# A two-layer decoder trunk on one core: gate and up products of an FFN chunk in a PSUM bank each

## The chip, the core and the metric

The kernel runs on one core of a Trainium2 chip. Five engines of the core work side by side, each on its own list of instructions: TensorE (PE; its weight loads are listed as PEld), VectorE (DVE), ScalarE (ACT), GpSimd (POOL) and SyncE (SP, which issues the DMAs). They meet at semaphores. Matmul results go to PSUM, which the program uses as eight banks of 512 fp32 columns by 128 partitions. The metric is the device time of one execution in microseconds; the median of three runs is 998.04 us (997.99 to 998.23).

## The reference

A trunk of two layers works on x of 256 rows by 1024 columns in fp32. Each layer is FFN, mixer, FFN, each with a scaled residual and a layer norm:

```
def swiglu(x, w_gu, w_down):
    g, u = jnp.split(x @ w_gu, 2, axis=-1)
    return (jax.nn.silu(g) * u) @ w_down

x = layer_norm(ALPHA * x + 0.5 * swiglu(x, ffn_w_gu[l, 0], ffn_w_down[l, 0]), ...)
y = mixer_ab(...) if l % 2 == 0 else mixer_c(...)
x = layer_norm(ALPHA * x + y, ...)
x = layer_norm(ALPHA * x + 0.5 * swiglu(x, ffn_w_gu[l, 1], ffn_w_down[l, 1]), ...)
```

The FFN width is 2816: gate and up are 1024 x 2816 each, down is 2816 x 1024. The first mixer is attention beside a spatial gating unit, the second an mLSTM. The four FFNs are what the change touches.

## The kernel before, in words

Every fp32 operand of a large product is split into a high part (fp32r) and the rest, and a product is three matmuls, high by high, high by rest, rest by high (mm3, lines 119 to 122). Weights come from HBM as pages of 128 x 1024 fp32 (512 KB): SP loads a page into one of 6 raw buffers, ACT casts it to whi (line 92), DVE subtracts to get wlo (line 93), and both parts lie in rings of 9 pages. When TensorE is done with page n, w_done (line 86) splits page n + 9 and loads page n + 15.

An FFN begins with two or four tiles of 128 rows by 512 columns (gate 256, up 256), which are transposed afterwards (post, line 314). All the other columns go in chunks of 128 (chunk, line 327): 20 chunks in the first FFN, 18 in each of the others, 74 together. A chunk computes its gate product transposed, 128 columns by all 256 rows, with 8 x 3 = 24 matmuls out of one weight page (proj_t, line 255), then its up product with 24 more out of the next page. ACT takes Silu of the gate (line 332), DVE multiplies it by the up product (line 334), and ACT and DVE split the result hT into its two parts. Then come the down products into four banks with the tag a (out_proj, line 265) and the layer norm.

PSUM has three pools: four banks with the tag a, three with the tag m, one with the tag t. A tile of tag m is taken by bank_m (line 51), in turn; a tile takes a bank again when all readers of the bank's last tile are done. Gate and up of a chunk are the two halves of one such tile.

The code is written in one order, but a scheduler of the framework sets the order on each engine except SP (line 36): it lays the instructions out by priority and its own costs, and so may put matmuls of the next chunk ahead of those which it believes to wait. It also sets the semaphore waits, and treats two engines at one PSUM bank as dependent, also where they touch different columns.

Of the kernel before, what the change touches and what calls it, by code (L numbers as in the profile page):

```python
# [10 lines left out]
AF = mybir.ActivationFunctionType  # L11
OP = mybir.AluOpType
AX = mybir.AxisListType

P = 128
S = 256
# [14 lines left out]
def trunk(ctx, tc, W, xT_d, x_d, g_d, b_d, rope_d, id_d, idb_d, mk_d, tri_d, sel_d,  # L31
          sg_d, sb_d, sw_d, sbt_d, cw_d, wif_d, bif_d, hg_d, out_d):
    nc = tc.nc
# [11 lines left out]
    def bank(tag, bufs, shape=(P, 512), dt=F32):  # L45
        return psum.tile(list(shape), dt, tag=tag, name="ps_" + tag, bufs=bufs)
# [4 lines left out]
    def bank_m(shape=(P, 512)):  # L51
        return bank("m", 3, shape)

    def bank_t(shape=(P, 512)):
        return bank("t", 1, shape)

    def page(name, shape, dt=F32):
        n = 1
        for d in shape[1:]:
            n *= d  # L60
        v = pages.tile([P, 516], dt, tag="p2", name=name, bufs=PAGES)[:, 0:n]
        if len(shape) == 3:
            v = v.rearrange("p (a b) -> p a b", a=shape[1])
        elif len(shape) == 4:
            v = v.rearrange("p (a b c) -> p a b c", a=shape[1], b=shape[2])
        return v
# [19 lines left out]
    def w_done(n):  # L86
        del whi[n], wlo[n]
        w_split(n + RING)
        w_dma(n + RING + RAW)

    def split(src, hi, lo):
        nc.scalar.copy(out=hi, in_=src)  # L92
        nc.vector.tensor_tensor(out=lo, in0=src, in1=hi.bitcast(F32), op=OP.subtract)  # L93
# [3 lines left out]
    def spawn(gen):  # L97
        side.append([0, gen])
        return gen
# [7 lines left out]
    def tick():  # L107
        for e in list(side):
            e[0] -= 1
            if e[0] <= 0:  # L110
                step(e)

    def finish(gen):
        for e in list(side):
            if e[1] is gen:
                while e in side:
                    step(e)

    def mm3(out, lh, ll, rh, rl, start, stop):
        mm_(out=out, lhsT=lh, rhs=rh, start=start, stop=False)  # L120
        mm_(out=out, lhsT=lh, rhs=rl, start=False, stop=False)  # L121
        mm_(out=out, lhsT=ll, rhs=rh, start=False, stop=stop)  # L122
# [67 lines left out]
    def load_consts():  # L190
        nc.sync.dma_start(out=identb, in_=idb_d)
        nc.sync.dma_start(out=maskb, in_=mk_d)
        nc.sync.dma_start(out=tri, in_=tri_d)
        nc.sync.dma_start(out=sel, in_=sel_d)
        nc.sync.dma_start(out=cw, in_=cw_d)
        nc.sync.dma_start(out=bif, in_=bif_d)
# [44 lines left out]
    def proj(t, n0, release, out=None, js=range(4)):  # L241
        ps = out if out is not None else bank_m()
        for j in js:
            rh = whi[n0 + j].rearrange("p (a n) -> p a n", a=2)
            rl = wlo[n0 + j].rearrange("p (a n) -> p a n", a=2)
            for i in range(2):
                kc = 2 * j + i
                mm3(ps, xTh[:, kc, t * P:(t + 1) * P], xTl[:, kc, t * P:(t + 1) * P],
                    rh[:, i, :], rl[:, i, :], kc == 0, kc == 7)
            if release:  # L250
                w_done(n0 + j)
            tick()
        return ps

    def proj_t(n, ps):
        wh = whi[n].rearrange("p (k n) -> p k n", k=KC)
        wl = wlo[n].rearrange("p (k n) -> p k n", k=KC)
        for kc in range(KC):
            mm3(ps, wh[:, kc, :], wl[:, kc, :], xTh[:, kc, :], xTl[:, kc, :], kc == 0, kc == 7)
            if kc == 3:  # L260
                tick()
        w_done(n)
        tick()

    def out_proj(nk, n0, lhs, skew, k, scale, eps, last):
        acc = [[None, None], [None, None]]

        def one(c, t, release, hs=(0, 1)):
            n = n0 + c
            lh, ll = lhs(c, t)  # L270
            for h in hs:
                if acc[t][h] is None:
                    acc[t][h] = bank_a()
            for h in hs:
                mm3(acc[t][h], lh, ll, whi[n][:, h * 512:(h + 1) * 512], wlo[n][:, h * 512:(h + 1) * 512],
                    c == 0, c == nk - 1)
            if release:
                w_done(n)
            if 1 in hs:
                tick()  # L280

        for c in range(nk - skew):
            one(c, 0, False)
            one(c, 1, True)
        for c in range(nk - skew, nk):
            one(c, 0, False, (0,))
        ln0 = layer_norm(0, acc[0], scale, eps, k, last)
        next(ln0)
        for c in range(nk - skew, nk):
            one(c, 0, False, (1,))  # L290
        spawn(ln0)
        if last:
            segs = ((0, 512), (512, 256), (768, 256))
            accs = [acc[1][0], acc[1][1], bank_m()]
            ln1 = layer_norm(1, accs, scale, eps, k, last, segs)
            for i, (o, w) in enumerate(segs):
                for c in range(nk - skew, nk):
                    n = n0 + c
                    lh, ll = lhs(c, 1)
                    mm3(accs[i][:, 0:w], lh, ll, whi[n][:, o:o + w], wlo[n][:, o:o + w],  # L300
                        i == 2 and c == nk - skew, c == nk - 1)
                next(ln1)
            finish(ln0)
            return spawn(ln1)
        for c in range(nk - skew, nk):
            one(c, 1, True)
        finish(ln0)
        return spawn(layer_norm(1, acc[1], scale, eps, k, last))

    def ffn(n0, k, ln_prev, last=False):  # L310
        hT = {}
        head = 1 if ln_prev is None else 2

        def post(g, t, ps):
            hp = pages.tile([P, 2, 256], F32, tag="h", name="hp", bufs=3)
            nc.scalar.activation(out=hp[:, 0, :], in_=ps[:, 0:256], func=AF.Silu)
            nc.vector.tensor_tensor(out=hp[:, 1, :], in0=hp[:, 0, :], in1=ps[:, 256:512], op=OP.mult)
            yield 2
            pt = bank_t((P, 2, P))
            for c in range(2):  # L320
                nc.tensor.transpose(pt[:, c, :], hp[:, 1, c * P:(c + 1) * P], ident)  # L321
            q = page("hT", [P, 2, 2, P], F32R)
            for c in range(2):
                hT[2 * g + c, t] = (q[:, 0, c, :], q[:, 1, c, :])
            split(pt, q[:, 0], q[:, 1])

        def chunk(c):
            n = n0 + 4 * head + 2 * (c - 2 * head)
            ps = bank_m()
            hp = pages.tile([P, 2, 256], F32, tag="h", name="hp", bufs=3)  # L330
            proj_t(n, ps[:, 0:256])
            nc.scalar.activation(out=hp[:, 0, :], in_=ps[:, 0:256], func=AF.Silu)  # L332
            proj_t(n + 1, ps[:, 256:512])
            nc.vector.tensor_tensor(out=hp[:, 1, :], in0=hp[:, 0, :], in1=ps[:, 256:512], op=OP.mult)  # L334
            q = page("hT", [P, 2, S], F32R)
            split(hp[:, 1, :], q[:, 0], q[:, 1])
            for t in range(2):
                w = slice(t * P, (t + 1) * P)
                hT[c, t] = (q[:, 0, w], q[:, 1, w])

        if ln_prev is None:
            load_consts()
        gens = []
        if ln_prev is None:
            order = []
            ps = [bank_m(), bank_m()]
            for j in range(4):
                proj(0, n0, False, ps[0], (j,))
                proj(1, n0, True, ps[1], (j,))
            for t in range(2):  # L350
                gens.append(spawn(post(0, t, ps[t])))
        else:
            order = [(0, 0), (1, 0), (0, 1), (1, 1)]
        for g, t in order:
            if (g, t) == (0, 1) and ln_prev is not None:
                finish(ln_prev)
            ps = proj(t, n0 + 4 * g, t == 1)
            gens.append(spawn(post(g, t, ps)))
        for c in range(2 * head, FC):
            chunk(c)  # L360

        def lhs(c, t):
            if (c, t) not in hT:
                for e in gens:
                    finish(e)
            return hT[c, t]

        return out_proj(FC, n0 + 4 * FG, lhs, 7, k, 2.0 * ALPHA, 4.0 * EPS, last)
# [478 lines left out]
```

## Time and profile before

| | |
|---|---|
| median of 3 runs | 998.04 us |
| profiled execution, its own time | 998.46 us |
| its span | 996.5 us |
| PE busy | 981.1 us (98%) |
| DVE, ACT busy | 596.0 us (60%), 458.4 us (46%) |
| DMA | 183.01 MB, mean 184 GB/s |

The span runs from the first to the last instruction of the profile. Busy time of PE is the union of drawn matmuls, whose ends are modelled, so a matmul is drawn longer than the distance to the next one's start. Where PE loses time is seen in the distances between starts and in the idle time of PEld, the weight load ahead of each matmul.

### The profile page before, as it was taken

To read this page: it belongs to the slowest core of one execution; us is meant where nothing else is said; L and a number is where in the kernel's file an instruction comes from. 1 tells how busy PE (TensorE), PEld (TensorE's weight loads), DVE (VectorE), ACT (ScalarE), POOL (GpSimd) and SP (SyncE) were. 2 spreads that over 40 slices of the span, in tenths; PEclk is the share of its full clock that TensorE was granted. 3 is DMA by queue.
4 is the path that set the end of the run, shared out by engine and by line. 5 is a ranking of instruction groups with operands and counts; after the bars stand their busy time and mean duration, and the time that the engine had idled before them with its cause. 6 is when DMAs were issued, how large, how long until landed. Compare 5 with 4: busy or idle time off the path is not lost.

```text
span 996.5 us, 15539 instructions
## 1 busy us (share of the span) xinstructions
PE 981.1 (98%) x6212; PEld 863.5 (87%) x6212; DVE 596.0 (60%) x822; ACT 458.4 (46%) x664; POOL 23.8 (2%) x36
## 2 busy tenths in 40 slices
PE   8999999999999999999999999999999999999997
PEld 5999998887788999988889999888888789999886
DVE  5575554586768655554675555448767885555434
ACT  5464443346645444443354444324675454444420
POOL 0000000010000000000000000001000000000000
PEclk9999999999999999999999999999999999999999
DMA  8885556386336655566565555655634466555611
GB/s 298 295 277 180 181 186 192 118 284 199 118 113 225 215 187 184 176 190 190 166 221 182 180 183 170 194 186 198 209 125 130 136 225 212 184 171 179 197 48 42
DMA packets 52215, 183.01 MB, mean 184 GB/s; under 512 B 6192, under 2 KB 6832, under 8 KB 52016
## 3 DMA queue, kind: packets, MB, share of 16 engines
q1 hardware_dynamic: 52144, 182.04, 56.5%
q8 instruction: 48, 0.79, 0.3%
q14 instruction: 23, 0.19, 0.1%
HBM read 180.97 MB, written 1.05 MB: 183 GB/s over the span
## 4 chain that ended last, share of the span: by engine, by line
PE 94%; DVE 2%; issue 1%; ACT 1%; DMA 1%; POOL 0%; SPq 0%; DVEq 0%; ACTq 0%
PE ps_m L120 22%; PE ps_m L121 20%; PE ps_m L122 20%; PE ps_a L121 10%; PE ps_a L120 9%; PE ps_a L122 9%; DVE wlo L93 1%; PE ps_a L232 1%; DMA raw<-in_W 1%; PE ps_a L428 1%; POOL hrs L201 0%; ACT whi L92 0%; PE ps_a L465 0%; PE ps_t L321 0%; ACT hp L332 0%
## 5 line engine op out<-in xcount | busy, mean ns | idle before, releaser
L92 ACT CAST whi<-raw 128x1024 fp32r<-128x1024 f32 (+1 forms) x325 | 339.9, 1050 | 402.7 <-PE ps_m L121 227.1
L93 DVE TENSOR_TENSOR wlo<-raw,whi 128x1024 fp32r<-128x1024 f32 (+1 forms) x325 | 394.5, 1221 | 153.6 <-ACT whi L92 151.7
L120 PE MATMUL ps_m<-xTh,whi 128*128 128x256 f32 x1280 | 366.4, 286 | 3.1 <-DVE qkc L637 1.4
L121 PE MATMUL ps_m<-xTl,whi 128*128 128x256 f32 x1280 | 357.6, 280 | 0.0
L122 PE MATMUL ps_m<-xTh,wlo 128*128 128x256 f32 x1280 | 347.2, 279 | 0.0
L120 PEld LDWEIGHTS ps_m<-xTh,whi 128*128 128x128 f32 x1280 | 240.4, 188 | 18.6 <-ACT hp L332 16.2
L121 PEld LDWEIGHTS ps_m<-xTl,whi 128*128 128x128 f32 x1280 | 240.7, 188 | 0.4 <-issue 0.2
L122 PEld LDWEIGHTS ps_m<-xTh,wlo 128*128 128x128 f32 x1280 | 236.3, 188 | 0.3 <-issue 0.3
L120 PE MATMUL ps_a<-whi,hT 128*128 128x512 f32 (+1 forms) x352 | 138.2, 393 | 0.0
L121 PE MATMUL ps_a<-wlo,hT 128*128 128x512 f32 (+1 forms) x352 | 138.1, 392 | 0.0
L122 PE MATMUL ps_a<-whi,hT 128*128 128x512 f32 (+1 forms) x352 | 137.9, 392 | 0.0
L334 DVE TENSOR_TENSOR hp<-hp,ps_m 128x256 f32<-128x256 f32 x74 | 31.2, 421 | 159.3 <-PE ps_m L122 159.3
L120 PE MATMUL ps_m<-whi,xTh 128*128 128x512 f32 x240 | 98.3, 411 | 2.6 <-ACT whi L92 2.5
L121 PE MATMUL ps_m<-wlo,xTh 128*128 128x512 f32 x240 | 96.7, 403 | 0.5 <-DVE wlo L93 0.5
L122 PE MATMUL ps_m<-whi,xTl 128*128 128x512 f32 x240 | 95.9, 400 | 0.0
L122 PEld LDWEIGHTS ps_a<-whi,hT 128*128 128x128 f32 x352 | 66.1, 188 | 15.2
L120 PEld LDWEIGHTS ps_a<-whi,hT 128*128 128x128 f32 x352 | 66.1, 188 | 14.9
L121 PEld LDWEIGHTS ps_a<-wlo,hT 128*128 128x128 f32 x352 | 66.2, 188 | 14.8
L120 PEld LDWEIGHTS ps_m<-whi,xTh 128*128 128x128 f32 x240 | 45.7, 191 | 13.3 <-ACT whi L92 3.8
L121 PEld LDWEIGHTS ps_m<-wlo,xTh 128*128 128x128 f32 x240 | 45.9, 191 | 10.8 <-DVE wlo L93 1.2
L122 PEld LDWEIGHTS ps_m<-whi,xTl 128*128 128x128 f32 x240 | 45.7, 190 | 10.5
L210 DVE SCALAR_TENSOR_TENSOR xn<-xn,ps_a 128x512 f32<-128x512 f32 x24 | 16.0, 684 | 37.0 <-PE ps_a L122 36.9
(189 smaller groups left out, 583.2 us busy)
## 6 DMA issues: line engine op xcount, KB each, us to landing
raw<-in_W SPq DMA_DIRECT2D x323, 512.0 KB, 4.3
gb<-in_g SPq DMA_DIRECT2D x6, 512.0 KB, 4.2
gb<-in_b SPq DMA_DIRECT2D x6, 512.0 KB, 5.1
xn<-in_x SPq DMA_DIRECT2D x1, 1024.0 KB
out<-xn SPq DMA_DIRECT2D x4, 256.0 KB, 2.1
xt<-in_xT SPq DMA_DIRECT2D x3, 256.0 KB, 7.6
raw<-in_W SPq DMA_DIRECT2D x2, 256.0 KB, 3.5
swt<-in_sw SPq DMA_DIRECT2D x2, 256.0 KB, 7.9
```

The lines of the kernel that those rows point to most:

```text
L92: nc.scalar.copy(out=hi, in_=src)
L93: nc.vector.tensor_tensor(out=lo, in0=src, in1=hi.bitcast(F32), op=OP.subtract)
L120: mm_(out=out, lhsT=lh, rhs=rh, start=start, stop=False)
L121: mm_(out=out, lhsT=lh, rhs=rl, start=False, stop=False)
L122: mm_(out=out, lhsT=ll, rhs=rh, start=False, stop=stop)
L210: nc.vector.scalar_tensor_tensor(out=sl, in0=sl, scalar=scale, in1=acc[i], op0=OP.mult, op1=OP.add)
L232: nc.tensor.transpose(pt[:, c, :], sl[:, c * P:(c + 1) * P], ident)
L334: nc.vector.tensor_tensor(out=hp[:, 1, :], in0=hp[:, 0, :], in1=ps[:, 256:512], op=OP.mult)
L428: mm_(out=dst, lhsT=qk[0, t][:, c, :], rhs=kp[c][:, :, 0:nk * P], start=True, stop=False, skip_group_check=True)
```

## The change

A chunk takes two tiles of the tag m in place of one, each of 128 partitions by 256 columns, the gate product in the first, the up product in the second. Silu and the multiplication read the new tiles. The pool still has three banks. Line numbers behind the change move: the multiplication on line 334 becomes line 335.

```
         def chunk(c):
             n = n0 + 4 * head + 2 * (c - 2 * head)
-            ps = bank_m()
             hp = pages.tile([P, 2, 256], F32, tag="h", name="hp", bufs=3)
-            proj_t(n, ps[:, 0:256])
-            nc.scalar.activation(out=hp[:, 0, :], in_=ps[:, 0:256], func=AF.Silu)
-            proj_t(n + 1, ps[:, 256:512])
-            nc.vector.tensor_tensor(out=hp[:, 1, :], in0=hp[:, 0, :], in1=ps[:, 256:512], op=OP.mult)
+            pg = bank_m((P, S))
+            proj_t(n, pg)
+            nc.scalar.activation(out=hp[:, 0, :], in_=pg, func=AF.Silu)
+            pu = bank_m((P, S))
+            proj_t(n + 1, pu)
+            nc.vector.tensor_tensor(out=hp[:, 1, :], in0=hp[:, 0, :], in1=pu, op=OP.mult)
```

On TensorE, within the second FFN, this is where a gate product of before gives way to the up product of its chunk. ps_m_3364 is the bank of one chunk, ps_m_3431 that of the next; whi_3157 and whi_3170 are the gate and up pages of the first, whi_3185 the gate page of the second, and the number behind a wait means nothing here.

```order
L122 MATMUL ps_m_3364<-xTh_72,wlo_3158 128x256
L120 MATMUL ps_m_3431<-xTh_72,whi_3185 128x256 [waits DVE_49]
L121 MATMUL ps_m_3431<-xTl_73,whi_3185 128x256
...
L120 MATMUL ps_m_3431<-xTh_72,whi_3185 128x256
L121 MATMUL ps_m_3431<-xTl_73,whi_3185 128x256
L120 MATMUL ps_m_3364<-xTh_72,whi_3170 128x256 [waits Activation_49]
L121 MATMUL ps_m_3364<-xTl_73,whi_3170 128x256
```

Eleven matmuls of the next chunk's gate stand between, of which two are shown at the start and two at the end. Then the first up matmul waits for ACT, and the rest of the next gate product, 13 matmuls, follows the up product.

The same place on TensorE after the change: ps_m_3387 is the gate tile of a chunk, ps_m_3419 its up tile, ps_m_3455 the gate tile of the next chunk.

```order
L121 MATMUL ps_m_3387<-xTl_73,whi_3177 128x256
L122 MATMUL ps_m_3387<-xTh_72,wlo_3178 128x256
L120 MATMUL ps_m_3419<-xTh_72,whi_3190 128x256 [waits Activation_49]
L121 MATMUL ps_m_3419<-xTl_73,whi_3190 128x256
...
L121 MATMUL ps_m_3419<-xTl_73,whi_3190 128x256
L122 MATMUL ps_m_3419<-xTh_72,wlo_3191 128x256
L120 MATMUL ps_m_3455<-xTh_72,whi_3205 128x256 [waits DVE_49]
L121 MATMUL ps_m_3455<-xTl_73,whi_3205 128x256
```

Nothing stands between gate and up any more. Each product is 24 matmuls in a row, through all four FFNs, and the first of a product carries a wait, for ACT in an up product and for DVE in a gate product.

On ACT, of before, the same chunk and the one ahead of it: hp is Silu's output, whi a weight page, hT the chunk's result.

```order
L332 ACTIVATE hp_3298<-ps_m_3297 128x256 [waits PE_49,Activation_49]
L92 CAST whi_3354<-raw_3189 128x1024 [waits DMAHW4_49,PE_49]
L92 CAST hT_3361<-hp_3298 128x256 [waits DVE_49]
L92 CAST whi_3390<-raw_3201 128x1024 [waits DMAHW5_49,PE_49]
L332 ACTIVATE hp_3365<-ps_m_3364 128x256 [waits PE_49,Activation_49]
```

And after the change:

```order
L332 ACTIVATE hp_3318<-ps_m_3319 128x256 [waits PE_49,Activation_49]
L92 CAST whi_3376<-raw_3209 128x1024 [waits DMAHW4_49,PE_49]
L92 CAST hT_3383<-hp_3318 128x256 [waits DVE_49]
L92 CAST whi_3412<-raw_3221 128x1024 [waits DMAHW5_49,PE_49]
L332 ACTIVATE hp_3386<-ps_m_3387 128x256 [waits PE_49,Activation_49]
```

The sequence on ACT is the same: a page cast stands ahead of each Silu. Outside the four stretches of chunks no engine's order differs.

## Rows read from the trace of the kernel before

**Rows 1.** The page, parts 1 and 2: TensorE, its clock, DMA rate.

```profile
PE 981.1 (98%) x6212; PEld 863.5 (87%) x6212; DVE 596.0 (60%) x822; ACT 458.4 (46%) x664; POOL 23.8 (2%) x36
...
PEclk9999999999999999999999999999999999999999
...
GB/s 298 295 277 180 181 186 192 118 284 199 118 113 225 215 187 184 176 190 190 166 221 182 180 183 170 194 186 198 209 125 130 136 225 212 184 171 179 197 48 42
```

**Rows 2.** Chunk stretches: us; busy us (instructions) by engine; clock; DMA share; GB/s.

```profile
22.49:142.11 119.62, 119.16 (x970) 115.19 (x969) 70.07 (x87) 59.08 (x88) 0.00 (x0) 1.00 0.68 223
325.34:433.04 107.70, 107.32 (x872) 103.33 (x871) 58.24 (x74) 48.68 (x73) 0.00 (x0) 1.00 0.59 187
517.73:625.32 107.59, 107.17 (x873) 103.20 (x872) 58.20 (x74) 48.64 (x73) 0.00 (x0) 1.00 0.60 188
821.29:928.91 107.62, 107.22 (x873) 103.24 (x872) 58.24 (x74) 48.64 (x73) 0.00 (x0) 1.00 0.60 188
```

**Rows 3.** Weight load's waits: us in total, times, longest.

```profile
PEld ps_m L120 <- ACT hp L332: 16.2, 69, 0.4
PEld ps_m L120 <- ACT whi L92: 3.8, 3, 2.9
```

**Rows 4.** Timeline of TensorE, second stretch: start us, us drawn, what.

```profile
336.01 0.28 PE L121 MATMUL ps_m<-xTl,whi 128*128 128x256 f32 x1
...
338.58 0.40 PE L122 MATMUL ps_m<-xTh,wlo 128*128 128x256 f32 x2
338.81 0.28 PE L120 MATMUL ps_m<-xTh,whi 128*128 128x256 f32 x1
...
341.38 0.28 PE L121 MATMUL ps_m<-xTl,whi 128*128 128x256 f32 x1
341.68 0.38 PE L120 MATMUL ps_m<-xTh,whi 128*128 128x256 f32 x1
341.90 0.28 PE L121 MATMUL ps_m<-xTl,whi 128*128 128x256 f32 x1
```

**Rows 5.** Timeline of the weight load there; idle before, and its releaser.

```profile
341.67 0.19 PEld L120 LDWEIGHTS ps_m<-xTh,whi 128*128 128x128 f32 x1 [0.22 <-ACT hp L332]
```

**Rows 6.** Timeline of ACT there.

```profile
340.29 1.05 ACT L92 CAST whi<-raw 128x1024 fp32r<-128x1024 f32 x1 [0.16 <-PE ps_m L121]
341.25 0.37 ACT L332 ACTIVATE hp<-ps_m 128x256 f32<-128x256 f32 x1
```

**Rows 7.** Timeline of TensorE, last chunk of the third stretch.

```profile
622.00 0.40 PE L121 MATMUL ps_a<-wlo,hT 128*128 128x512 f32 x1
622.23 0.40 PE L122 MATMUL ps_a<-whi,hT 128*128 128x512 f32 x1
622.52 0.39 PE L120 MATMUL ps_m<-xTh,whi 128*128 128x256 f32 x1
622.74 0.28 PE L121 MATMUL ps_m<-xTl,whi 128*128 128x256 f32 x1
```

**Rows 8.** Timeline of DVE, second stretch.

```profile
327.77 0.42 DVE L317 TENSOR_TENSOR hp<-hp,ps_m 128x256 f32<-128x256 f32 x1
...
338.96 0.42 DVE L334 TENSOR_TENSOR hp<-hp,ps_m 128x256 f32<-128x256 f32 x1 [2.25 <-PE ps_m L122]
339.87 1.23 DVE L93 TENSOR_TENSOR wlo<-raw,whi 128x1024 fp32r<-128x1024 f32 x1 [0.48 <-ACT whi L92]
```

**Rows 9.** Timeline of DVE in the mLSTM stage.

```profile
717.35 1.51 DVE L637 SCALAR_TENSOR_TENSOR qkc<-ps_m,cw,qkc 128x255 f32<-128x255 f32 x3
```

**Rows 10.** Timeline of TensorE at that time, first and last of 27.

```profile
717.56 0.28 PE L120 MATMUL ps_m<-xTh,whi 128*128 128x256 f32 x1
...
720.59 0.28 PE L122 MATMUL ps_m<-xTh,wlo 128*128 128x256 f32 x1
```

**Rows 11.** Waits within 325 to 433 us.

```profile
ACT whi L92 <- PE ps_m L121: 55.4, 33, 3.1
```

**Rows 12.** A stretch at the start; columns as in rows 2.

```profile
13.48:16.45 2.97, 2.97 (x8) 2.29 (x7) 2.72 (x3) 2.35 (x4) 0.00 (x0) 0.50 1.03 414
```

## The prediction

> **What bounds the kernel now.** I read the page first. TensorE is busy for 981.1 of 996.5 us, at a granted clock of 9 tenths or more in every slice [rows 1]. No other engine is near that, so a change counts if it alters how densely TensorE's stream is packed. The busy share can't say how dense it is, since each matmul is drawn 0.28 us long while the next one starts 0.12 us later. Starts must be read instead.
>
> Next I read the four stretches in which the chunks of the four FFNs run [rows 2]. They take 119.62, 107.70, 107.59 and 107.62 us, 442.5 us together, all at a clock of 1.00, with DVE busy 54 to 59% and ACT 45 to 49%.
>
> Then the waits of TensorE's weight load, over the whole span. By far the longest is for ACT's line 332, the Silu of a chunk: 16.2 us in 69 waits, against 3.8 for the next in the list [rows 3]. There are 74 chunks (20, 18, 18, 18). Silu reads columns 0 to 255 of the bank and the waiting matmul writes columns 256 to 511, so no number passes between them; what they share is the bank.
>
> Last, the stream around one such wait [rows 4]. From the matmul after one wait (336.01) to the matmul after the next (341.90) is 5.89 us for the 48 matmuls of a chunk. The 46 pitches up to 341.38 take 5.37 us, 0.1167 each. The last two take 0.30 and 0.22 us, 0.52 in place of 0.233. The weight load shows 0.22 us of idle, released by line 332 [rows 5]; the rest of the loss is in the matmul behind it, which starts 0.22 us later although its own load took only 0.19: the load that normally lies under earlier matmuls had nothing to lie under. So one wait costs 0.52 - 0.233 = 0.287 us, more than its idle row.
>
> Why Silu is late although eleven matmuls of the next gate product are put in between: on ACT the cast of a weight page (1.05 us from 340.29) stands ahead of it, and Silu starts only at 341.25 [rows 6].
>
> **The change, part by part.**
>
> It removes the second half of the bank as the place of the up product, and with it the dependency on Silu. In the order of the changed program the up product is no longer split off behind eleven matmuls of the next gate product. It follows its gate product directly, and 24 stands behind 24 through all four stretches. The Activation wait still written on the first up matmul is not for this chunk's Silu: the bank it takes was last read by the Silu of the chunk before, a whole up product plus a gate product earlier.
>
> - Sum of the waits removed: 69 x 0.287 = 19.8 us.
> - The last chunk of each FFN has its up product behind six down-projection matmuls. There 622.23 to 622.74 is 0.51 us in place of 0.233 + 0.117 [rows 7], a loss of 0.16 which the waits don't list. It goes too; four times, 0.6 us.
> - Together 20.4 us.
>
> It adds no instruction. Matmuls, casts, Silus, products, table loads and DMAs stand in the same numbers as before, and the orders of ACT and DVE in the steady part are the same sequence: page cast, Silu, page cast, cast of hT on ACT.
>
> It adds a change of bank between gate and up. The stream of before already changes banks inside the fill at no price: at 338.58 the last up matmul and the next gate matmul start within 0.23 us, the ordinary pitch [rows 4]. I cost it at nothing.
>
> It adds a wait for a free bank. Three banks used to hold three chunks and now hold one and a half. The gate of chunk c+2 takes the bank of the up product of chunk c, which DVE's product (line 334 of before) must have read. That product starts at 338.96 and takes 0.42 us, done 0.8 us after the last up matmul's start at 338.58 [rows 4, 8]. In the new order 48 matmuls (5.6 us) lie between. Slack 4.8 us, so I cost it at nothing. Were it used up, the gate product would wait with all of TensorE's queue behind it.
>
> It lets DVE and ACT read one chunk bank while TensorE writes its neighbour. The same form is already in the trace. In the mLSTM stage products of 128x256 get a bank each from the same pool, and while three DVE reads run from 717.35 to 718.86, TensorE goes from 717.56 to 720.59 in 26 pitches of 0.1165 us [rows 9, 10], the same pitch as in the FFN stream. So neither the read nor the neighbouring write slows the stream there.
>
> Faster chunks ask for weights sooner: 2 pages, 1.05 MB, per 5.60 us is 187 GB/s. The start of the span moves 277 to 298 GB/s [rows 1]. In the second stretch ACT's casts wait 55.4 us for TensorE to release a page slot [rows 11], so the ring is full and the weights are ahead. Nothing.
>
> Bounds of the gain. From below the idle rows alone, if the late second matmul has some other cause: 16.2 us. From above the stretches as a whole: in the second, 864 x 0.1167 + 6 x 0.233 + about 0.3 for two transposes, less the last pitch, is 102.4 of 107.70 us, so 5.3 can go; likewise 5.7 in the first and 5.2 in each of the others, 21.4 together. I take 20.4, which counts only what I can put at a named wait.
>
> The sum: the profiled execution took 998.46 us (span 996.5). 998.46 - 20.4 = 978.06, span about 976.1. The median of the runs is 998.04, 0.42 lower, so 977.6.
>
> A rule that speaks against the change: the Trainium skill, "TensorE: Matmul & The Clock Gate", section "A second HAM failure mode: psum-queue depth-cycling", says that a kernel which moves to another PSUM bank in each iteration can leave TensorE so many short pauses that its clock keeps dropping back. This change doubles the moves. The trace doesn't bear the rule out so far: moves between three banks are there already, and the clock stands at 1.00 in all four stretches. I give it a place among the rivals.
>
> **The rivals.**
>
> 1. *The product on DVE becomes the wait (slower).* With only one and a half chunks of banks, the gate of chunk c+2 waits on DVE. For it: DVE works in order, and a page subtraction of 1.23 us can stand just ahead of the product [rows 8]. Against: it would have to end 4.8 us later than now. It turns the gain into a loss once the wait exceeds 20.4 / 74 = 0.28 us a chunk, that is once the product ends 5.9 us after its up product's last start. At 1 us beyond the slack: 977.6 + 74 = 1052 us.
>
> 2. *The two tiles land in one bank, so the change doesn't do what it says.* A tile of 256 columns needs half a bank; if the pool packed two together, the wait would stay at the same 0.287 us: 998 us. Against: [rows 9, 10], where such tiles of this pool are read and written at the same time without a wait.
>
> 3. *The clock falls in the chunk stretches (slower).* At the low level (0.50, 1.2 GHz) eight matmuls of 512 columns start within 2.97 us, 0.424 apart [rows 12], against 0.233, so one of 256 columns would start about 0.096 later (estimate: half the difference). The gain is gone after 20.4 / 0.096 = 212 of the 3552 chunk matmuls; with a tenth of them at that level, 977.6 + 34 = 1012 us. Against: the change takes pauses away and adds none that I find.
>
> 4. *Part of the gain meets another wait.* The denser stream meets a weight page, a transpose or a cast a little late, once or twice in each FFN. Only the idle rows go: 998.0 - 16.2 = 981.8 us. For it: in the second stretch the last tile ahead of the chunks is read by DVE until 328.19 [rows 8], 2.9 us into the stretch, and in the new order its bank is asked for at 325.34 + 48 x 0.1167 = 330.9, a slack of 2.7 us where the steady part has 4.8. Against: the same-pitch stretches above, and ACT's idle time ahead of its casts.
>
> **How the numbers follow.** Forecast 0.90 (about 975.5 to 980), rival 4 0.05, rival 1 0.02, rival 2 0.02, rival 3 0.01. The range from 975.5 to 982 reaches from a little past the upper bound of the gain to its lower bound, and leaves out the three rare rivals and some of the forecast's tails. What the measurement of this kernel can tell from no change is about 0.2%, 2 us. Faster by more: forecast and rival 4, 0.95. Within it: rival 2, 0.02. Slower: rivals 1 and 3, 0.03.
>
> **What would show it.** In the changed profile: no wait of the weight load for line 332 within the chunk stretches; Silu to Silu 5.60 us in place of 5.89; the four stretches at about 114 and three times 102.5 us; line 122 to line 120 at 0.117 from gate to up; DVE's product still read within a microsecond of its up product. The out-projections and mixers keep their lengths, since their order is unchanged. Wrong would be a new wait of TensorE for DVE's product (rival 1), the same 69 waits (rival 2), a granted clock below 1.00 in a stretch (rival 3), or a pitch above 0.117 while ACT reads the neighbouring bank, which I hold to be free from one place of the trace.

## The result, and the profile after

The changed kernel took 975.8 us in the median of four runs (975.12 to 976.97), the kernel before 998.02 (997.99 to 998.23): a ratio of 0.978, 95% interval 0.976 to 0.980. The forecast of 977.6 was 1.8 us too slow; the measured time lies in its range, 0.3 us above the lower end. The profiled execution of the changed kernel took 976.97 us with a span of 975.0, 21.5 less than the span before.

The page, TensorE and its clock, to be read against [rows 1] (busy us, share, instructions):

```profile
span 975.0 us, 15544 instructions
...
PE 960.9 (99%) x6212; PEld 858.1 (88%) x6212; DVE 598.7 (61%) x822; ACT 458.8 (47%) x664; POOL 23.9 (2%) x36
...
PEclk9999999999999999999999999999999999999999
```

By this line every engine has the same number of instructions as before. Only TensorE's busy time changed by much, by 20 us, although its work is the same. The matmuls are drawn 0.28 us long, so the late starts of 0.22 to 0.30 us left hardly a gap, and the busy share of 98% had not shown that there was something to gain.

The chunks' four stretches, with the columns of [rows 2] (length, busy time and instructions of PE, PEld, DVE, ACT, POOL, granted clock, DMA share, GB/s):

```profile
22.77:135.30 112.53, 112.53 (x964) 112.35 (x963) 70.79 (x87) 59.29 (x88) 0.00 (x0) 1.00 0.71 237
319.87:420.79 100.92, 100.92 (x867) 100.92 (x866) 58.89 (x74) 48.76 (x73) 0.00 (x0) 1.00 0.63 200
506.82:607.73 100.91, 100.91 (x866) 100.91 (x865) 58.86 (x74) 48.74 (x73) 0.00 (x0) 1.00 0.64 201
805.11:906.03 100.92, 100.92 (x866) 100.92 (x865) 58.88 (x74) 48.71 (x73) 0.00 (x0) 1.00 0.63 201
```

These end with the last chunk's matmul. Those of [rows 2] contain six down-projection matmuls too, which stood ahead of the last up product, 6 x 0.233 = 1.40 us. With that taken off, the stretches are 5.69, 5.38, 5.28 and 5.30 us shorter, 21.65 together: the whole gain of the span is in the chunks. The clock is 1.00 in each, and the weight load is now busy for all of a stretch, where it had idled for 4 us.

The weight load's waits, longest first (total us, times, longest; "issue" is idle time that no other engine is seen to end), against [rows 3]:

```profile
PEld ps_m L120 <- ACT whi L92: 4.1, 3, 2.9
PEld L145 <- issue: 1.9, 7, 0.3
```

The first line of before, 16.2 us for Silu in 69 waits, is gone and none took its place. What was second is now first, at about the same size (4.1 us for 3.8).

TensorE, ACT and DVE around one switch from gate to up in the second stretch (start us, us drawn, engine, line, what). TensorE:

```profile
339.59 0.28 PE L122 MATMUL ps_m<-xTh,wlo 128*128 128x256 f32 x1
339.70 0.28 PE L120 MATMUL ps_m<-xTh,whi 128*128 128x256 f32 x1
...
340.75 0.28 PE L120 MATMUL ps_m<-xTh,whi 128*128 128x256 f32 x1
340.87 0.28 PE L121 MATMUL ps_m<-xTl,whi 128*128 128x256 f32 x1
...
342.39 0.28 PE L122 MATMUL ps_m<-xTh,wlo 128*128 128x256 f32 x1
342.50 0.28 PE L120 MATMUL ps_m<-xTh,whi 128*128 128x256 f32 x1
...
345.30 0.28 PE L120 MATMUL ps_m<-xTh,whi 128*128 128x256 f32 x1
```

ACT, with the idle time before an instruction and its releaser in brackets:

```profile
339.79 1.05 ACT L92 CAST whi<-raw 128x1024 fp32r<-128x1024 f32 x1 [1.40 <-PE ps_m L121]
340.74 0.38 ACT L332 ACTIVATE hp<-ps_m 128x256 f32<-128x256 f32 x1
...
346.34 0.38 ACT L332 ACTIVATE hp<-ps_m 128x256 f32<-128x256 f32 x1
```

DVE:

```profile
342.77 0.42 DVE L335 TENSOR_TENSOR hp<-hp,ps_m 128x256 f32<-128x256 f32 x1 [0.68 <-PE ps_m L122]
```

The gate product ends with the matmul at 339.59, and the up product's first starts 0.11 us later. The page cast still stands ahead of Silu, which starts only at 340.74, 1.15 us after the gate's last matmul: as late as before, and nobody waits for it. While Silu reads the gate's bank until 341.12, the up product's matmuls in the neighbouring bank keep their 0.12 us. DVE reads the up product 0.38 us after the start of its last matmul (342.39). From up product to up product, 339.70 to 345.30, it is 5.60 us for the 48 matmuls, against 5.89 in [rows 4].

### The profile page after: what moved, and what is told of

Same layout as the page of the kernel before. It is cut to its first block, busy times and chain, and to the rows that moved or that the text cites. A ratio compares the mean times of both kernels' runs of the same rounds, so it can differ in the third digit from the quotient of the medians.

```text
span 975.0 us, 15544 instructions
## 1 busy us (share of the span) xinstructions
PE 960.9 (99%) x6212; PEld 858.1 (88%) x6212; DVE 598.7 (61%) x822; ACT 458.8 (47%) x664; POOL 23.9 (2%) x36
## 4 chain that ended last, share of the span: by engine, by line
PE 95%; DVE 2%; DMA 1%; ACT 0%; issue 0%; POOL 0%; SPq 0%; DVEq 0%
PE ps_m L121 21%; PE ps_m L122 21%; PE ps_m L120 21%; PE ps_a L121 10%; PE ps_a L120 10%; PE ps_a L122 10%; DVE wlo L93 1%; PE ps_a L232 1%; DMA raw<-in_W 1%; PE ps_a L429 1%; POOL hrs L201 0%; PE ps_a L466 0%; ACT whi L92 0%; PE ps_t L321 0%; PE ps_a L455 0%
## 5 line engine op out<-in xcount | busy, mean ns | idle before, releaser
L120 PE MATMUL ps_m<-xTh,whi 128*128 128x256 f32 x1280 | 358.2, 280 | 1.4 <-DVE qkc L638 1.4
L122 PE MATMUL ps_m<-xTh,wlo 128*128 128x256 f32 x1280 | 357.2, 279 | 0.0
L122 PEld LDWEIGHTS ps_m<-xTh,wlo 128*128 128x128 f32 x1280 | 240.6, 188 | 0.3 <-issue 0.3
```

## The experiments

The theory was that the whole gain is an uncovered wait for Silu at a shared bank. The rivals were that the bank's sharing costs something beyond that wait, that the cast ahead of Silu is the real cause, and that the ring of banks is close to its limit. Two experiments remove the wait in other ways than the change does, two change how often or how early it comes, one takes a bank away, and one measures the changed kernel again. Each ratio is to the kernel before in runs on the same chip, with its 95% interval.

### One bank, Silu behind the up product

```
-  nc.scalar.activation(out=hp[:, 0, :], in_=ps[:, 0:256], func=AF.Silu)
   proj_t(n + 1, ps[:, 256:512])
+  nc.scalar.activation(out=hp[:, 0, :], in_=ps[:, 0:256], func=AF.Silu)
```

> One bank per chunk as before, but Silu is issued after the up product, so the 48 matmuls of a chunk follow one another and no up product waits. Theory A (the gain is the removed wait for Silu at the shared bank, 0.29 us a chunk): as fast as the changed kernel, 975 to 978 us, no wait of the weight load for Silu, chunk stretches of about 112.5 and three times 101 us. Rival B (a bank of its own for each product makes the stream denser, for instance by the matmul pitch while another engine reads): about 998 us, or at least 2 us above the changed kernel, with a pitch of 0.1167 or more in place of 0.1165. Rival C (the page cast ahead of Silu is what costs): 975 to 978 us as well.

Measured: 976.76 us (976.39 to 976.89), ratio 0.979 (0.978 to 0.981). The second stretch (columns as above) and the longest wait of the weight load:

```profile
319.80:420.72 100.92, 100.92 (x866) 100.92 (x865) 58.89 (x74) 48.45 (x72) 0.00 (x0) 1.00 0.64 200
```

```profile
PEld ps_m L120 <- ACT whi L92: 3.8, 3, 1.8
```

The stretch has the length of the changed kernel, 100.92 us in both, with gate and up in the two halves of one bank. So one bank for both costs nothing that shows here. What cost was a reader of its first half that had to be done before its second half could be written.

### One bank, but a gate product in between

```
-        def chunk(c):
+        def gate(c):
...
-            proj_t(n, ps[:, 0:256])
+            proj_t(n0 + 4 * head + max(0, 2 * i - 1), ps[:, 0:256])
...
-            proj_t(n + 1, ps[:, 256:512])
+            return ps, hp
+
+        def up(c, ps, hp):
+            i, m = c - 2 * head, FC - 2 * head
+            proj_t(n0 + 4 * head + min(2 * i + 2, 2 * m - 1), ps[:, 256:512])
...
+        g = gate(2 * head)
...
-            chunk(c)
+            g1 = gate(c + 1) if c + 1 < FC else None
+            up(c, *g)
+            g = g1
```

The weight pages are stored in the order gate 0, gate 1, up 0, gate 2, up 1, and so on.

> One bank per chunk as before, but each chunk's gate product is placed ahead of the up product of the chunk before (the weight pages lie in that order), so a whole product, 2.8 us, lies between a gate product and its up product. The dependency on Silu stays. Theory A (what costs is a wait that isn't covered, not the shared bank): no wait of the weight load for Silu, 975 to 978 us. Rival B (two engines at one bank slow the stream): about 998 us, or a pitch of 117.0 ns or more in place of 116.7.

Measured: 976.79 us (975.56 to 977.99), ratio 0.979 (0.977 to 0.981). The second stretch, the longest wait of the weight load, and ACT around a Silu in that stretch:

```profile
320.31:421.23 100.92, 100.92 (x866) 100.92 (x865) 58.82 (x74) 48.74 (x73) 0.00 (x0) 1.00 0.65 200
```

```profile
PEld ps_m L120 <- ACT whi L92: 4.1, 3, 2.7
```

```profile
331.83 1.05 ACT L92 CAST whi<-raw 128x1024 fp32r<-128x1024 f32 x1 [1.45 <-PE ps_m L121]
332.79 0.38 ACT L332 ACTIVATE hp<-ps_m 128x256 f32<-128x256 f32 x1
```

The dependency is still there, the cast still stands ahead of Silu, and no wait for Silu is in the list: 24 matmuls, 2.8 us, cover what 11 did not. A third way to the same time.

### The change in every second chunk

```
   ps = bank_m()
+  pu = bank_m((P, S)) if c % 2 == 0 else ps[:, 256:512]
...
-  proj_t(n + 1, ps[:, 256:512])
+  proj_t(n + 1, pu)
```

37 of the 74 chunks have two banks.

> Two banks in every second chunk (37 of 74), one bank in the others. Theory A: half of the waits stay, 37 x 0.29 = 10.7 us are saved, about 987 us (985.5 to 988.5), with 34 to 37 waits of the weight load for Silu. Rival D (what is saved depends on the whole stream, since in a mixed order the remaining waits become longer or the chunk ahead fills them): 998 or 976 us, with waits of another length than 0.23 us.

Measured: 987.56 us (987.52 to 989.09), ratio 0.991 (0.989 to 0.992). The weight load's longest wait (Silu has line 333 here):

```profile
PEld ps_m L120 <- ACT hp L333: 8.7, 36, 0.4
```

Half of the waits are left with half of the idle time, and half of the gain: 10.1 us between the medians and 10.9 between the profiled spans (996.5 and 985.6) are 0.27 and 0.29 us for each changed chunk. The gain goes by the count of waits, with no sign of a part that comes once for the whole kernel.

### Silu ahead of the page cast

With False as its third argument proj_t leaves w_done and the last tick to its caller.

```
-  proj_t(n, ps[:, 0:256])
-  nc.scalar.activation(out=hp[:, 0, :], in_=ps[:, 0:256], func=AF.Silu)
+  proj_t(n, ps[:, 0:256], False)
+  si = nc.scalar.activation(out=hp[:, 0, :], in_=ps[:, 0:256], func=AF.Silu)
+  with tc.issue_after(si.ins):
+      w_done(n)
+  tick()
```

> One bank per chunk as before, but on ACT the cast of the page that the gate product releases is issued after Silu, not ahead of it; the scheduler now puts 4 matmuls of the next gate product into the gap in place of 11. Rival C (Silu comes late because of the cast, as the prediction put it): the wait all but goes, 976 to 982 us. Theory A' (the scheduler fills the gap to the end of Silu as it reckons it, and the chip is about 0.23 us later than that whatever stands ahead): the idle time per wait stays at 0.2 to 0.3 us, about 998 us (996 to 999).

Measured: 1000.24 us (999.26 to 1001.44), ratio 1.003 (1.002 to 1.004): slower by 0.3%, outside of what I expected. First the weight load's longest wait, then ACT, TensorE and the weight load around one of them:

```profile
PEld ps_m L120 <- ACT hp L333: 18.4, 69, 0.3
```

```profile
340.94 0.39 ACT L333 ACTIVATE hp<-ps_m 128x256 f32<-128x256 f32 x1 [1.18 <-PE ps_m L122]
341.22 1.04 ACT L92 CAST whi<-raw 128x1024 fp32r<-128x1024 f32 x1
```

```profile
340.56 0.28 PE L122 MATMUL ps_m<-xTh,wlo 128*128 128x256 f32 x1
340.68 0.28 PE L120 MATMUL ps_m<-xTh,whi 128*128 128x256 f32 x1
...
341.04 0.73 PE L120 MATMUL ps_m<-xTh,whi 128*128 128x256 f32 x2
```

```profile
341.38 0.19 PEld L120 LDWEIGHTS ps_m<-xTh,whi 128*128 128x128 f32 x1 [0.27 <-ACT hp L333]
```

The edit did what it says: ACT idles ahead of Silu, and Silu starts 0.38 us after the start of the gate's last matmul (340.56), the distance at which DVE read the up product above. Yet there are 69 waits again, each a little longer (18.4 / 69 = 0.27 us of idle, against 0.23). The scheduler, which sees Silu free earlier, now puts only four matmuls between gate and up (340.68 to 341.04; the second of the two in the last line is already the up product's) where it had put eleven. On the chip the up product's first weight load starts 0.82 us after the gate's last matmul, seven pitches of 0.117. In the kernel before it was the same with the cast in the sum: the load at 341.67 [rows 5] starts 1.57 us after the gate's last matmul (340.10, eleven pitches ahead of 341.38 in [rows 4]), 13.4 pitches, and there were eleven matmuls to fill them. So the fill falls two to three matmuls short with the cast and without it. That the scheduler fits the fill to an estimate of Silu's end, and that the estimate is short, is inferred from these two places; the estimate itself is in no row. Nor was the fill varied alone: eleven matmuls with Silu ahead of the cast, or three more with the cast ahead of it, were not run. The version with a whole gate product in between has 24, and no wait.

### The changed kernel with two banks of tag m

```
-  return bank("m", 3, shape)
+  return bank("m", 2, shape)
```

> The changed kernel with two banks of the tag m in place of three, everywhere. Now the gate product of chunk c+1 takes the bank whose Silu was read one product ago, and its up product the bank that DVE's product of chunk c must have read within one product, 24 matmuls or 2.8 us after the last up matmul. Theory A (the price of the change, fewer chunks in the banks, is nothing because DVE is done 0.8 us after the last up matmul's start): the three later chunk stretches stay at 101 us and no weight load waits for DVE's product; only the mixers may lose, up to 5 us; 975 to 981 us. The slower rival of the prediction (the product on DVE becomes the wait) would show here first: a wait in each chunk, 74 x 0.2 us or more, 990 us and above.

Measured: 983.2 us (981.89 to 984.44), ratio 0.985 (0.984 to 0.987): 0.6 to 0.8% slower than the changed kernel (976.35 in a second series, and 975.8), above the 975 to 981 that I expected. The second stretch, and then one of 19.78 us in the mLSTM and four pieces of it:

```profile
318.10:419.21 101.11, 101.11 (x866) 100.98 (x865) 58.98 (x74) 48.77 (x73) 0.00 (x0) 1.00 0.62 199
```

```profile
725.63:745.41 19.78, 15.75 (x112) 15.01 (x111) 14.30 (x33) 8.94 (x15) 2.31 (x2) 0.91 0.43 138
...
733.60:735.60 2.00, 0.04 (x1) 0.00 (x0) 2.00 (x3) 1.48 (x2) 0.00 (x0) 1.00 0.15 12
735.60:737.60 2.00, 0.63 (x4) 0.42 (x4) 1.96 (x4) 0.59 (x1) 0.00 (x0) 1.00 0.75 246
737.60:739.60 2.00, 1.30 (x6) 1.33 (x7) 1.97 (x6) 0.42 (x1) 0.00 (x0) 0.67 0.33 63
739.60:741.60 2.00, 2.00 (x11) 2.00 (x11) 0.46 (x2) 0.42 (x1) 0.00 (x0) 0.50 0.52 207
```

The same stretch of the changed kernel with three banks:

```profile
725.74:741.20 15.46, 14.02 (x112) 13.46 (x111) 13.81 (x31) 8.81 (x15) 2.31 (x2) 1.00 0.59 182
```

The chunks hardly need the third bank: with one chunk's worth of banks their stretch is 0.19 us longer, and no wait for DVE's product of a chunk appears. The loss is between the third and the fourth stretch, where the mLSTM runs, whose products of 128x256 take banks of the same tag. From stretch to stretch, with two banks and with three:

```profile
606.38:809.86 203.48, 197.31 (x995) 163.53 (x994) 135.65 (x220) 98.66 (x136) 9.85 (x10) 0.99 0.51 167
```

```profile
607.73:805.11 197.38, 195.22 (x996) 161.56 (x994) 135.33 (x220) 98.84 (x136) 9.83 (x10) 1.00 0.53 173
```

That is 6.1 us, of which 4.3 are in the piece above. The spans differ by less, 4.9 us, because this profiled execution, the fastest of its four, reached its first stretch 1.96 us earlier (at 20.81 us for 22.77). TensorE around the pause in the piece, with two banks:

```profile
735.87 0.63 PE L702 MATMUL ps_t<-ident,num 128*128 128x128 f32 x4 [2.23 <-DVE num L698]
738.30 0.55 PE L120 MATMUL ps_m<-xTh,whi 128*128 128x256 f32 x1 [1.80 <-DVE qkc L638]
738.65 0.42 PE L121 MATMUL ps_m<-xTl,whi 128*128 128x256 f32 x1
...
741.64 0.32 PE L120 MATMUL ps_m<-xTh,whi 128*128 128x256 f32 x1
```

And with three:

```profile
733.57 0.28 PE L120 MATMUL ps_m<-xTh,whi 128*128 128x256 f32 x1
...
736.26 0.28 PE L122 MATMUL ps_m<-xTh,wlo 128*128 128x256 f32 x1
736.38 0.60 PE L702 MATMUL ps_t<-ident,num 128*128 128x128 f32 x4
738.41 0.36 PE L120 MATMUL ps_m<-xTh,whi 128*128 128x256 f32 x1 [1.44 <-DVE qkc L638]
```

With three banks a product of 24 matmuls (733.57 to 736.26) stands ahead of the transposes on line 702, and the next one waits for DVE's line 638, which reads a product of tag m. With two banks nothing stands there: the transposes wait for their input from DVE, and the product waits for line 638 itself. So 24 matmuls, 2.8 us, move behind the pause. The order there was made anew for two banks, and that a bank held by DVE's reads is the reason for it is the likely reading, not shown by itself. After the pause the granted clock is 0.67 and then 0.50: the 14 matmuls from 738.65 to 741.64 start 0.214 us apart in place of 0.117, which is another 1.4 us. The two make up nearly all of the 4.3.

### The changed kernel once more

> The changed kernel once more, beside the others on their chip: 975 to 977 us, to tell the scatter of its runs (975.12 to 976.97) from a difference between kernels.

Measured: 976.35 us (975.92 to 978.01), ratio 0.979 (0.978 to 0.981), to the same runs of before (997.67) as the versions with Silu moved. The three versions without the wait (976.35, 976.76, 976.79) can't be told apart, and no experiment pointed to one faster than these.

## Why the prediction was right

**What bounds the kernel.** Right. The starts of TensorE's matmuls, not its busy share, showed the loss, and it was at one releaser.

**The sum.** The mechanism held; the term "69 x 0.287 + 0.6" was too small, 20.4 for 21.65 us in the stretches. Over all chunks it comes to 21.65 / 74 = 0.293 us. I priced every wait by one that I had picked, of 0.22 us of idle, while the mean over the 69 is 16.2 / 69 = 0.235. Counting the starts in the four stretches of before, 64 chunks have the form of [rows 4], a pair of late starts; they cost 0.293 each, 18.7 us. That is nearly my price. The other ten chunks, the four last ones and six others, most of them at the beginning of a stretch, gave up the remaining 2.9 us, 0.29 each, where I had 2.0 (5 x 0.287 + 0.6). Most of the miss is there. The other estimate, each stretch less its matmuls at full pitch, gave 5.7, 5.3, 5.2 and 5.2, and measured are 5.69, 5.38, 5.28 and 5.30. I used it as the upper bound, which the measured 21.65 passes by 0.25, and it was the better estimate: it needs no list of waits.

The forecast's remaining distance, 21.5 us between the spans and 22.2 between the medians, is scatter of the runs: the profiled execution of after lies 1.2 us above its median, that of before 0.4.

**Why Silu is late.** What [rows 6] show is so: the cast stands ahead of Silu. As the whole reason for the wait it fell. Without the cast the wait is as long (1000.24 us), with the cast and enough matmuls in between it is gone (976.79). What decides is whether the matmuls put between reach to Silu's end, and with four and with eleven they did not. Why the scheduler puts too few stays an inference. The sum did not rest on this point, so the time alone could not have shown it.

**A change of bank at no cost, and a neighbour's read at no cost.** Right: 0.11 us from gate to up, and the ordinary pitch while Silu reads. The bound on the bank from the mLSTM [rows 9, 10] carried over.

**The ring of banks.** Right, and with room: the slack was put at 4.8 us, and the chunks run nearly as well with two banks (101.11 for 100.92 us).

**Weights.** Right: the three later stretches move 200 GB/s, and the pages' casts still wait for TensorE (50.3 us in 35 waits between 319 and 421 us), not for data.

**The rivals.** DVE's product as the new wait did not come, not with two banks either. The two tiles did not share a bank, since the waits went. The clock stayed at 1.00 in all four stretches. But the change does not double TensorE's moves between banks, as I had put it: by the orders ahead of the prediction, 48 matmuls of before hold three moves (13 matmuls of one gate product, 11 of the next, 24 of an up product), and now two. So the result is no test of the rule of the Trainium skill that I had weighed ("TensorE: Matmul & The Clock Gate", section "A second HAM failure mode: psum-queue depth-cycling"); with three moves and with two the clock was at 1.00, and the rule is not seen. A clock that falls behind a pause is seen, in the run with two banks, and there the price that I had estimated for the low level, 0.096 us a matmul, was 0.097. No other wait took a part of the gain.

The same skill, "PSUM — Partial Sum Buffer", section "PSUM bank collisions raise a hardware error", says to guard PSUM by bank and not by address. The program of before is guarded so: 69 waits for a reader of other columns in the same bank, 0.29 us each. What happens without the guard, no run here shows.

## What to carry to other kernels

Under this framework a reader and the next writer of one PSUM bank run one after the other even where their columns differ; look for the wait, and then either give the writer another bank, or put enough of TensorE's own work between, or issue the reader later. The three are worth the same (975.8 to 976.8 us here), so take the one that costs no bank that another stage needs: a bank less of the tag m cost the mLSTM 6.1 us. And price such a change by the stretch less its matmuls at full pitch; the waits that the profile lists, 16.2 us here, were three quarters of what was to be had.

## What was not expected

Taking an instruction away from ahead of the awaited one made the kernel slower (0.3%), since the order was made anew around it, with four matmuls in the gap in place of eleven. Where a scheduler fills gaps by its own costs, an edit that makes the reader earlier can be spent by the fill; it was seen here once.

With two banks, a pause of TensorE (0.67 us of work in the 4 us from 733.6) was followed by a granted clock of 0.67 and then 0.50, the 1.2 GHz level, until about 741.6. So the price of the missing bank was more than the work that moved: of the 4.3 us some 1.4 are the clock's.
